# Feed-forward down products of a four-block network on one core: eight plain products per pair of blocks, or seven in Strassen's way

## Chip, cores and metric

The kernel runs on 1 core of one Trainium2 chip. The metric is the time of one execution on the device in microseconds; a comparison uses the median of the runs. Engines are named as the profile names them: PE (TensorE, matmuls), DVE (VectorE), ACT (ScalarE), POOL (GpSimd) and SP (SyncE, which issues the transfers here).

## What is computed

512 tokens of width 1024, float32, pass through two blocks of one kind (a mixer of three parts, layer norm, a feed-forward, layer norm) and two of another (feed-forward, attention mixer, feed-forward, gated side input, each with rms norms). The change concerns the feed-forwards alone:

```python
D_MODEL = 1024; D_FF = 4 * D_MODEL; D_FF_2 = 2816
# both layers of the first kind
h = layer_norm(DEEPNORM_ALPHA * h + mixed @ w_out[l], ln1_g[l], ln1_b[l])
ff = jnp.square(jax.nn.relu(h @ w_up[l])) @ w_down[l]
h = layer_norm(DEEPNORM_ALPHA * h + ff, ln2_g[l], ln2_b[l])
# twice in each layer of the second kind
def swiglu(x, wi, wo):
    gate, up = jnp.split(x @ wi, 2, axis=-1)
    return (jax.nn.silu(gate) * up) @ wo
```

So there are two feed-forwards of width 4096 (called FFN1 here) and four of width 2816 (FFN2(layer, first or second)).

## The kernel before, in words

**Products.** Every float32 operand of a matmul is split into a high part, rounded to the PE's float32r, and a low part, the difference; a product of two operands is three matmuls (`mm3`, L179 to L182): high x high, low x high, high x low. A weight tile of 128 x 1024 is a `unit` (L149 to L177): SP loads it into `raw`, ACT rounds it to `wh` (L143; with a gain vector L175), DVE makes `wl` (L144, or L176).

**Tokens.** The 512 tokens are four tiles t = 0 to 3. `h` and `acc` hold each as 128 x 1024. For an up product the input stands transposed in `xh`, `xl` (eight k tiles of 128 x 512 tokens): PE turns `h` against the identity into PSUM (`ax`, L255), ACT casts and DVE subtracts (L143, L144).

**FFN1** (`ffn1`, L449 on) goes through 8 groups of 512 hidden columns. `up` (L468 to L470) fills four PSUM banks; ACT applies Relu (L474), DVE squares (L475), and ACT and DVE split the result into `xh`, `xl` of a second transposed room. The down products of a group come one group later, while the next group's up products run: for each tile t and column half, 12 matmuls of 512 columns into one bank, which DVE adds to `acc` (L341; the first group takes the residual in, L359). The first group's up goes over the tokens in two halves (256 columns each), so that it can begin before the last two tiles are transposed. The last group's down goes tile by tile, and `done(t)` starts the norm of each tile as soon as it is there.

**FFN2** (`ffn2`, L495 on) is alike with 11 blocks of 256 hidden columns in groups [0], [1, 2], ... [9, 10]: up L516 to L518, Silu on ACT (L522), the product with the other half on DVE (L523).

**PSUM** has 8 banks: four `mm`, two `ax`, two `sx`. Weights rotate through 3 + 3 `raw` tiles and 4 + 2 pairs `wh`, `wl` inside the feed-forwards.

**Ends.** Behind an FFN2 `rms_add` (L430 to L438) computes `yg` = acc x gain on DVE, sums of squares on ACT (L402) and an inverse root in small DVE steps, then the new `h` in two halves (L437); `rms_T_late` transposes it. `ple` (L1252 on) is the gated side input: it loads `pt`, transposes it (L1261), and its gate is a down product of the whole `xh`, `xl` with `ple_gate_2`.

**Order.** The program is written in one sequence of operations; a list scheduler of the framework sets each engine's order from it, from dependencies and from the tiles' buffers. `issue_after` holds some weight splits back at a stage's start. So an order is known for each engine, and an instruction waits for semaphores in that order.

## Time and profile before

| | us |
|---|---|
| median of 3 runs (lowest, highest) | 3498.74 (3496.28, 3499.62) |
| the profiled execution's own time | 3504.65 |
| its span | 3502.9 |
| PE busy | 3444.0 (98%) |
| PE weight load busy | 2925.8 (84%) |
| DVE busy | 1843.2 (53%) |
| ACT busy | 1435.2 (41%) |
| DMA engines, mean busy share | 27.8% |

The span runs from the first to the last instruction of the profiled execution. Busy time adds up the durations of an engine's instructions, one on another counted once; matmuls overlap, so that a row's mean duration is not the distance of two starts. A group's idle time is that of its engine just before it, with what ended it. The chain of waits is followed back from the last instruction.

### The profile page before, as it was taken

To read this page: it belongs to the slowest core of one execution; us is meant where nothing else is said; L and a number is where in the kernel's file an instruction comes from. 1 tells how busy PE (TensorE), PEld (TensorE's weight loads), DVE (VectorE), ACT (ScalarE), POOL (GpSimd) and SP (SyncE) were. 2 spreads that over 40 slices of the span, in tenths; PEclk is the share of its full clock that TensorE was granted. 3 is DMA by queue.
4 is the path that set the end of the run, shared out by engine and by line. 5 is a ranking of instruction groups with operands and counts; after the bars stand their busy time and mean duration, and the time that the engine had idled before them with its cause. 6 is when DMAs were issued, how large, how long until landed. Compare 5 with 4: busy or idle time off the path is not lost.

```text
span 3502.9 us, 46155 instructions
## 1 busy us (share of the span) xinstructions
PE 3444.0 (98%) x17870; PEld 2925.8 (84%) x17870; DVE 1843.2 (53%) x4034; ACT 1435.2 (41%) x2529; POOL 11.2 (0%) x40
## 2 busy tenths in 40 slices
...
DMA packets 230512, 300.17 MB, mean 86 GB/s; under 512 B 23258, under 2 KB 148732, under 8 KB 230292
## 3 DMA queue, kind: packets, MB, share of 16 engines
q1 hardware_dynamic: 229716, 297.22, 27.8%
...
q14 instruction: 80, 0.66, 0.1%
q10 hardware_dynamic: 576, 0.00, 0.0%
...
## 4 chain that ended last, share of the span: by engine, by line
PE 92%; DVE 5%; ACT 2%; issue 1%; DMA 0%; SPq 0%; DVEq 0%; ACTq 0%
PE mm L180 14%; PE mm L181 14%; PE mm L182 14%; PE mm L516 9%; PE mm L517 9%; PE mm L518 9%; PE mm L469 3%; PE mm L470 3%; PE mm L468 3%; PE o L1014 2%; PE o L1148 1%; PE tp L609 1%; PE s L595 1%; PE o L1230 1%; PE ax L255 1%
## 5 line engine op out<-in xcount | busy, mean ns | idle before, releaser
L180 PE MATMUL mm<-wh,xh 128*128 128x512 f32 (+4 forms) x2496 | 939.6, 377 | 6.7 <-ACT wh L143 2.5
L181 PE MATMUL mm<-wh,xl 128*128 128x512 f32 (+4 forms) x2496 | 937.7, 376 | 0.0
L182 PE MATMUL mm<-wl,xh 128*128 128x512 f32 (+4 forms) x2496 | 937.7, 376 | 0.0
L144 DVE TENSOR_TENSOR wl<-raw,wh 128x1024 fp32r<-128x1024 f32 (+4 forms) x304 | 355.0, 1170 | 542.7 <-ACT wh L143 532.1
L143 ACT CAST wh<-raw 128x1024 fp32r<-128x1024 f32 (+4 forms) x304 | 306.3, 1009 | 758.9 <-PE mm L181 320.6
L175 ACT ACTIVATE wh<-raw,gT 128x512 fp32r<-128x512 f32 (+2 forms) x504 | 329.4, 697 | 618.3 <-issue 254.8
L516 PE MATMUL mm<-xh,wh 128*128 128x512 f32 (+1 forms) x1536 | 570.7, 373 | 2.2 <-ACT rl L522 1.6
L517 PE MATMUL mm<-xl,wh 128*128 128x512 f32 (+1 forms) x1536 | 571.9, 373 | 0.0
L518 PE MATMUL mm<-xh,wl 128*128 128x512 f32 (+1 forms) x1536 | 570.2, 373 | 1.3 <-DVE wl L176 1.3
L176 DVE SCALAR_TENSOR_TENSOR wl<-raw,gT,wh 128x512 fp32r<-128x512 f32 (+2 forms) x504 | 348.1, 723 | 423.2 <-ACT wh L175 422.6
L180 PEld LDWEIGHTS mm<-wh,xh 128*128 128x128 f32 x2496 | 473.8, 190 | 81.2 <-ACT xh L143 6.6
L181 PEld LDWEIGHTS mm<-wh,xl 128*128 128x128 f32 x2496 | 473.9, 190 | 71.4 <-DVE xl L144 1.0
L182 PEld LDWEIGHTS mm<-wl,xh 128*128 128x128 f32 x2496 | 473.3, 190 | 71.3 <-issue 1.4
L341 DVE TENSOR_TENSOR acc<-acc,mm 128x512 f32<-128x512 f32 x316 | 216.3, 685 | 244.8 <-PE mm L182 243.7
L516 PEld LDWEIGHTS mm<-xh,wh 128*128 128x128 f32 x1536 | 289.6, 189 | 54.5 <-ACT rl L522 2.4
L517 PEld LDWEIGHTS mm<-xl,wh 128*128 128x128 f32 x1536 | 290.9, 189 | 50.4 <-DVE xl L144 0.4
L518 PEld LDWEIGHTS mm<-xh,wl 128*128 128x128 f32 x1536 | 290.1, 189 | 51.3 <-DVE wl L176 1.5
L469 PE MATMUL mm<-xl,wh 128*128 128x512 f32 (+1 forms) x576 | 210.4, 366 | 1.5 <-DVE xl L144 1.5
L470 PE MATMUL mm<-xh,wl 128*128 128x512 f32 (+1 forms) x576 | 209.2, 366 | 0.1
L468 PE MATMUL mm<-xh,wh 128*128 128x512 f32 (+1 forms) x576 | 208.7, 366 | 0.0
L143 ACT CAST xh<-rl 128x512 fp32r<-128x512 f32 x152 | 93.4, 619 | 92.8 <-DVE rl L523 61.0
L469 PEld LDWEIGHTS mm<-xl,wh 128*128 128x128 f32 x576 | 108.6, 188 | 19.6 <-DVE xl L144 2.3
...
## 6 DMA issues: line engine op xcount, KB each, us to landing
...
raw<-ffn_wo SPq DMA_DIRECT2D x88, 512.0 KB, 3.8
raw<-w_up SPq DMA_DIRECT2D x64, 512.0 KB, 3.8
raw<-w_down SPq DMA_DIRECT2D x64, 512.0 KB, 3.7
...
raw<-w_out SPq DMA_DIRECT2D x16, 512.0 KB, 3.7
raw<-a_wqkv SPq DMA_DIRECT2D x16, 512.0 KB, 3.6
raw<-ple_gate SPq DMA_DIRECT2D x16, 512.0 KB, 3.6
```

The source lines that it names most:

```text
L143: act.copy(h, src)
L144: dve.tensor_tensor(l, src, h, OP.subtract)
L175: act.activation(wh[:, sl], v[:, sl], AF.Copy, scale=gv)
L176: dve.scalar_tensor_tensor(wl[:, sl], v[:, sl], gv, wh[:, sl], op0=OP.mult, op1=OP.subtract)
L180: pe.matmul(ps, sh, mh, start=start, stop=False)
L181: pe.matmul(ps, sl, mh, start=False, stop=False)
L182: pe.matmul(ps, sh, ml, start=False, stop=stop)
L469: pe.matmul(o, wh[:, j, fs_], xl, start=False, stop=False)
L470: pe.matmul(o, wl[:, j, fs_], xh, start=False, stop=k == 7)
L516: pe.matmul(o, wh[:, j, fs_], xh, start=k == 0, stop=False)
L517: pe.matmul(o, wh[:, j, fs_], xl, start=False, stop=False)
L518: pe.matmul(o, wl[:, j, fs_], xh, start=False, stop=k == 7)
```

## The change

Two blocks of 256 hidden columns make a pair, and a pair's down product is one product of block matrices, 2 x 2: token halves (tiles 0, 1 and 2, 3) by the two K halves of each block, times K halves by column halves of `w_down` or `ffn_wo_2`. `down7` computes it as seven products p1 to p7 of 12 matmuls each and not eight. The sums on the activations' side (S1 to S4) are four DVE operations of 256 columns per hidden tile pair and block (`pair_parts`, L474 to L477), the sums on the weights' side four of 1024 columns per pair (`minus`, L505, tiles `wt`), and each of the seven weight operands is split. p1 and p6 stay in the `ax` and `sx` banks over all pairs, p5 is summed in SBUF (`v5`); `share` adds the three into `acc` at the end. The other four products are added to `acc` per pair. A pair's down comes right behind its own up products.

FFN1: up goes by blocks of 256 (two PSUM banks, units of four k tiles x 256), the square is on ACT, 14 blocks go in seven pairs, the last two plainly in `last_group` (tiles 0, 1, then 2, 3, each pair over both blocks). FFN2: block 0 plain, 1 to 8 in four pairs, 9 and 10 in `last_group`. The extra room holds 3 pairs `wh`, `wl` and not 2. `ple` keeps its transposed side input in the room of `v5` and a `raw` tile. The counts of matmul instructions in the whole kernel go from 16826 to 16370: 360 fewer of 512 columns in the down products, and FFN1's two first up blocks as 192 of 256 and 96 of 512 columns where 384 of 256 stood, in each.

```diff
-XRAW, XWHL = 3, 2
+XRAW, XWHL = 3, 3
...
+    SLOT = 7 * 256
+    A12, A22, A11, S2, S3, S4, S1 = range(0, SLOT, 256)
...
+    def pair_parts(slot, ra, rb):
+        one, two = slice(0, 256), slice(256, 512)
+        split(*slot(A11, A11 + 256), ra[:, one])
+        split(*slot(A12, A12 + 512), rb)
+        dve.tensor_tensor(rb[:, two], rb[:, two], ra[:, two], OP.add)
+        dve.tensor_tensor(ra[:, two], ra[:, one], ra[:, two], OP.subtract)
+        dve.tensor_tensor(ra[:, one], rb[:, two], ra[:, one], OP.subtract)
+        dve.tensor_tensor(rb[:, one], rb[:, one], ra[:, one], OP.subtract)
+        split(*slot(S2, S2 + 512), ra)
+        split(*slot(S4, S4 + 512), rb)
...
+        return {1: [axt("p1", ax), axt("p1", ax)], 6: [axt("p6", sx), axt("p6", sx)], 5: v5, "begun": False}
...
+        def minus(x, y):
+            v = t_p.tile([128, 1024], F32, tag="t4", name="wt")
+            dve.tensor_tensor(v, x, y, OP.subtract)
+            return v
...
+        b11 = raw(0, 0)
+        u11 = parts(b11)
+        b21 = raw(1, 0)
+        u21 = parts(b21)
+        b12 = raw(0, 1)
+        t1 = minus(b12, b11)
+        b22 = raw(1, 1)
+        t2 = minus(b22, t1)
+        ut2 = parts(t2)
+        p2 = [mmt(), mmt()]
+        for i in range(2):
+            product(A11, u11, V[1], [i], not begun, last)
+            if i == 0:
+                product(S2, ut2, V[6], [i], not begun, last)
+            product(A12, u21, p2, [i])
+        product(S2, ut2, V[6], [1], not begun, last)
+        to_acc(p2, 0, 0)
+        ut1 = parts(t1)
+        p5 = [mmt(), mmt()]
+        product(S1, ut1, p5, (0, 1))
+        for tt in range(2):
+            v = V[5][:, tt]
+            if begun:
+                dve.tensor_tensor(v, v, p5[tt], OP.add)
+            else:
+                act.copy(v, p5[tt])
+        t4 = minus(b21, t2)
+        ut4 = parts(t4)
+        p4 = [mmt(), mmt()]
+        product(A22, ut4, p4, (0, 1))
+        to_acc(p4, 2, 0)
+        t3 = minus(b22, b12)
+        ut3 = parts(t3)
+        p7 = [mmt(), mmt()]
+        product(S3, ut3, p7, (0, 1))
+        to_acc(p7, 2, 1)
+        u22 = parts(b22)
+        p3 = [mmt(), mmt()]
+        product(S4, u22, p3, (0, 1))
+        to_acc(p3, 0, 1)
...
+    def last_group(hid, w, row0, done):
+        us = {(cc, u): unit(dap(w, (row0 + u * 256) * D + cc * 512, [[D, 128], [128 * D, 2], [1, 512]]), (2, 512))
+              for u in range(2) for cc in range(2)}
+        for t0 in (0, 2):
+            steps = [(t, cc) for t in (t0, t0 + 1) for cc in range(2)]
+            pss = {s: axt() if t0 == 0 and i < 2 else mmt() for i, s in enumerate(steps)}
+            for u in range(2):
+                for t, cc in steps:
+                    wh, wl = us[cc, u]
+                    for f in range(2):
+                        hh, hl = hid[2 * u + f]
+                        mm3(pss[t, cc], hh[:, t * 128:(t + 1) * 128], hl[:, t * 128:(t + 1) * 128],
+                            wh[:, f], wl[:, f], u + f == 0, u + f == 2)
+                    if u:
+                        sl = slice(cc * 512, cc * 512 + 512)
+                        dve.tensor_tensor(acc[t][:, sl], acc[t][:, sl], pss[t, cc], OP.add)
+                        if cc:
+                            done(t)
...
-        G = FF1 // 512
-        prev = None
-        for g in range(G):
-            cur = up(g, 2 if g == 0 else 1)
-            run_later()
-            if prev is not None:
-                dn(g - 1, prev)
-            prev = cur
-        dn(G - 1, prev)
...
+                act.activation(rl, rl, AF.Square)
...
+        for b in range(0, NB - 2, 2):
+            pair_parts(slot(0), *up(b, 1 if b else 2))
+            if not b:
+                run_later()
+            pair_parts(slot(1), *up(b + 1, 1))
+            V = V or sums(v5)
+            down7([slot(0), slot(1)], wd, (b, b + 1), V, init, b == NB - 4)
+        hid = [plain(i, r) for i, r in enumerate(up(NB - 2, 1))]
+        share(V, True)
+        hid += [plain(2 + i, r) for i, r in enumerate(up(NB - 1, 1))]
+        last_group(hid, wd, (NB - 2) * 256, done)
...
+        hid0 = [plain(4 + i, r) for i, r in enumerate(up(0, 2))]
+        V = None
+        for c in range(1, NB - 2, 2):
+            pair_parts(slot(0), *up(c, 1))
+            if c == 1:
+                for f in down_steps(hid0, wd, 0, True, False, init_copy, None, banks=[axt, axt]):
+                    f()
+                for t in (2, 3):
+                    dve.tensor_tensor(acc[t][:, 0:512], acc[t][:, 0:512], acc[t][:, 512:1024], OP.subtract)
+            pair_parts(slot(1), *up(c + 1, 1))
+            V = V or sums(v5)
+            down7([slot(0), slot(1)], wd, (c, c + 1), V, None, c == NB - 4)
+        hid = [plain(i, r) for i, r in enumerate(up(NB - 2, 1))]
+        share(V, False)
+        hid += [plain(2 + i, r) for i, r in enumerate(up(NB - 1, 1))]
+        last_group(hid, wd, (NB - 2) * 256, done)
...
-        pT = (ep.tile([128, 2, S], F32R, name="pTh"), ep.tile([128, 2, S], F32R, name="pTl"))
+        pT = (room.tile([128, 2, S], F32R, tag="v5", name="pTh"),
+              raw_tile(F32R).rearrange("p (k s) -> p k s", k=2))
```

In the listings below `h_97` to `h_100` are the tiles t = 0 to 3, `h<-h,g` multiplies a tile by the gain or adds the bias, `gv` is the transposed result with gain and bias, `bn`, `mv`, `rs...` are the norm's statistics.

**DVE at the start of layer 1's FFN1**, around the norm of the last tile. Before:

```order
L386 TENSOR_TENSOR h_99<-h_99,g_8591 128x1024 [waits DVE_49]
L199 SCALAR_TENSOR_TENSOR rsb_8814<-rsy_8813,rsp_8815 128x1 [waits DVE_49]
L204 SCALAR_TENSOR_TENSOR rsy_8813<-rsb_8814,rsy_8813 128x1 [waits DVE_49]
L199 SCALAR_TENSOR_TENSOR rsb_8814<-rsy_8813,rsq_8816 128x1 [waits DVE_49]
L204 SCALAR_TENSOR_TENSOR rsy_8813<-rsb_8814,rsy_8813 128x1 [waits DVE_49]
L379 TENSOR_SCALAR h_100<-acc_7953,mv_8807,rsy_8813 128x1024 [waits DVE_49]
L144 TENSOR_TENSOR wl_8968<-raw_8965,wh_8967 128x1024 [waits DMAHW5_49]
L144 TENSOR_TENSOR wl_9126<-raw_9123,wh_9125 128x1024 [waits DMAHW7_49]
L385 TENSOR_TENSOR h_100<-h_100,g_8589 128x1024 [waits DVE_49,PE_49]
L144 TENSOR_TENSOR xl_96<-gv_8830,xh_95 128x4x128 [waits Activation_49]
```

Now:

```order
L144 TENSOR_TENSOR wl_9184<-raw_9181,wh_9183 128x1024 [waits DMAHW4_49]
L208 SCALAR_TENSOR_TENSOR rsy_8985<-rsb_8986,rsy_8985 128x1 [waits DVE_49]
L505 TENSOR_TENSOR wt_9278<-raw_9276,raw_9264 128x1024 [waits DMAHW6_49,DMAHW0_49]
L203 SCALAR_TENSOR_TENSOR rsb_8986<-rsy_8985,rsq_8988 128x1 [waits DVE_49]
L505 TENSOR_TENSOR wt_9282<-raw_9280,wt_9278 128x1024 [waits DMAHW1_49,DVE_49]
L208 SCALAR_TENSOR_TENSOR rsy_8985<-rsb_8986,rsy_8985 128x1 [waits DVE_49]
L383 TENSOR_SCALAR h_100<-acc_8125,mv_8979,rsy_8985 128x1024 [waits DVE_49]
L144 TENSOR_TENSOR wl_9214<-raw_9211,wh_9213 128x1024 [waits DMAHW5_49]
L144 TENSOR_TENSOR wl_9267<-raw_9264,wh_9266 128x1024
L389 TENSOR_TENSOR h_100<-h_100,g_8761 128x1024 [waits DVE_49,PE_49]
L144 TENSOR_TENSOR wl_9273<-raw_9270,wh_9272 128x1024 [waits DMAHW7_49]
L144 TENSOR_TENSOR xl_96<-gv_9002,xh_95 128x4x128 [waits Activation_49]
```

A weight split of the second up block and two weight sums of the first pair stand ahead of `h_100`, and three weight splits, not two, between it and its first `xl`.

**PE at the passage from FFN2(0,1) to `ple(0)`**; `mm_20635` is the third product of the gate and `mm_21202` the first. Before, in the gate's third product:

```order
L180 MATMUL mm_20635<-wh_20606,xh_95 128x512
L255 MATMUL ax_20534<-cst_91,h_100 128x128 [waits DVE_49,PE_49]
L255 MATMUL ax_20534<-cst_91,h_100 128x128 x3
L1261 MATMUL ax_20573<-cst_91,pt_20569 128x128 [waits DMAHW7_49,PE_49]
L1261 MATMUL ax_20573<-cst_91,pt_20569 128x128
L255 MATMUL ax_20541<-cst_91,h_100 128x128 [waits DVE_49]
L255 MATMUL ax_20541<-cst_91,h_100 128x128 x3
L1261 MATMUL ax_20573<-cst_91,pt_20569 128x128 x2
L1261 MATMUL ax_20580<-cst_91,pt_20569 128x128 [waits PE_49]
L1261 MATMUL ax_20580<-cst_91,pt_20569 128x128 x3
L181 MATMUL mm_20635<-wh_20606,xl_96 128x512
```

Now, from the second turn of `h_99` on, which follows the last down product but for `h_99`'s first turn:

```order
L259 MATMUL ax_21089<-cst_91,h_99 128x128 [waits DVE_49,PE_49]
L259 MATMUL ax_21089<-cst_91,h_99 128x128 x3
L259 MATMUL ax_21150<-cst_91,h_100 128x128 [waits DVE_49,PE_49]
L259 MATMUL ax_21150<-cst_91,h_100 128x128 x3
L259 MATMUL ax_21157<-cst_91,h_100 128x128 [waits DVE_49,PE_49]
L259 MATMUL ax_21157<-cst_91,h_100 128x128 x3
L1423 MATMUL ax_21186<-cst_91,pt_21182 128x128 [waits DMAHW3_49,PE_49]
L1423 MATMUL ax_21186<-cst_91,pt_21182 128x128 x3
L1423 MATMUL ax_21193<-cst_91,pt_21182 128x128 [waits PE_49]
L1423 MATMUL ax_21193<-cst_91,pt_21182 128x128 x3
L184 MATMUL mm_21202<-wh_21205,xh_95 128x512 [waits Activation_49]
```

The gate's products stood around the transposes of `h_100` and `pt`, and now stand behind all of them.

**DVE behind the last up block of a pair**, FFN1 of layer 1; `rl` are the hidden values, `xl` with `rl` their low parts. Before, a group of 512 columns:

```order
L475 TENSOR_TENSOR rl_9091<-rl_9091 128x512 [waits Activation_49]
L475 TENSOR_TENSOR rl_9096<-rl_9096 128x512 [waits Activation_49]
L144 TENSOR_TENSOR wl_9279<-raw_9276,wh_9278 128x1024 [waits DMAHW3_49,PE_49,Activation_49]
L144 TENSOR_TENSOR xl_8857<-rl_9091,xh_8856 128x512 [waits Activation_49]
L144 TENSOR_TENSOR xl_8857<-rl_9096,xh_8856 128x512 [waits Activation_49]
L475 TENSOR_TENSOR rl_9101<-rl_9101 128x512 [waits Activation_49]
L475 TENSOR_TENSOR rl_9106<-rl_9106 128x512 [waits Activation_49]
L144 TENSOR_TENSOR xl_8857<-rl_9101,xh_8856 128x512 [waits Activation_49]
L144 TENSOR_TENSOR xl_8857<-rl_9106,xh_8856 128x512 [waits Activation_49]
```

Now, the pair's second block:

```order
L144 TENSOR_TENSOR xl_9029<-rl_9558,xh_9028 128x256 [waits Activation_49]
L144 TENSOR_TENSOR wl_9705<-raw_9592,wh_9704 128x1024 [waits PE_49,Activation_49]
L144 TENSOR_TENSOR xl_9029<-rl_9561,xh_9028 128x512 [waits Activation_49]
L474 TENSOR_TENSOR rl_9561<-rl_9561,rl_9558 128x256 [waits DVE_49]
L475 TENSOR_TENSOR rl_9558<-rl_9558 128x256 [waits DVE_49]
L476 TENSOR_TENSOR rl_9558<-rl_9561,rl_9558 128x256 [waits DVE_49]
L477 TENSOR_TENSOR rl_9561<-rl_9561,rl_9558 128x256 [waits DVE_49]
L144 TENSOR_TENSOR xl_9029<-rl_9558,xh_9028 128x512 [waits Activation_49]
L144 TENSOR_TENSOR xl_9029<-rl_9561,xh_9028 128x512 [waits Activation_49]
```

The squares are gone from DVE; between the first parts and the sums stand a weight split and the four sums, and the parts made of sums come last.

## Rows read from the trace of the kernel before

**Rows 1.** Page, span, busy time by engine, and the chain's shares by engine.

```profile
span 3502.9 us, 46155 instructions
PE 3444.0 (98%) x17870; PEld 2925.8 (84%) x17870; DVE 1843.2 (53%) x4034; ACT 1435.2 (41%) x2529; POOL 11.2 (0%) x40
...
PE 92%; DVE 5%; ACT 2%; issue 1%; DMA 0%; SPq 0%; DVEq 0%; ACTq 0%
```

**Rows 2.** Table by stage, feed-forwards: length, busy PE, PEld, DVE, ACT, POOL, clock, DMA share, GB/s.

```profile
317.00:675.00 358.00, 356.79 (x1675) 298.16 (x1673) 188.02 (x261) 119.31 (x172) 1.44 (x5) 1.00 0.31 95
...
sum 2188.00, PE 2182.23 PEld 1826.15 DVE 1043.15 ACT 765.85 POOL 1.77; mean PE 363.71 PEld 304.36 DVE 173.86 ACT 127.64 POOL 0.29
```

**Rows 3.** Page, costliest groups: matmul and weight load of line 180.

```profile
L180 PE MATMUL mm<-wh,xh 128*128 128x512 f32 (+4 forms) x2496 | 939.6, 377 | 6.7 <-ACT wh L143 2.5
...
L180 PEld LDWEIGHTS mm<-wh,xh 128*128 128x128 f32 x2496 | 473.8, 190 | 81.2 <-ACT xh L143 6.6
```

**Rows 4.** Timeline of PE in an FFN1 up stream: start, duration, instruction.

```profile
1482.69 0.39 PE L516 MATMUL mm<-xh,wh 128*128 128x512 f32 x1
1482.92 0.39 PE L517 MATMUL mm<-xl,wh 128*128 128x512 f32 x1
...
1483.37 0.39 PE L516 MATMUL mm<-xh,wh 128*128 128x512 f32 x1
```

**Rows 5.** Groups by shape, DVE, then ACT: busy us, mean ns, idle before.

```profile
L176 DVE SCALAR_TENSOR_TENSOR wl<-raw,gT,wh 128x512 fp32r<-128x512 f32 x440 | 314.3, 748 | 379.8 <-ACT wh L175 379.6
L144 DVE TENSOR_TENSOR wl<-raw,wh 128x1024 fp32r<-128x1024 f32 x256 | 312.9, 1224 | 482.1 <-ACT wh L143 476.3 <-DMA g<-ln_b 1.7 <-PE mm L182 0.6
L341 DVE TENSOR_TENSOR acc<-acc,mm 128x512 f32<-128x512 f32 x316 | 216.3, 685 | 244.8 <-PE mm L182 243.7
L144 DVE TENSOR_TENSOR xl<-rl,xh 128x512 fp32r<-128x512 f32 x152 | 104.1, 688 | 38.4 <-ACT xh L143 37.1
...
L143 ACT CAST wh<-raw 128x1024 fp32r<-128x1024 f32 x256 | 269.4, 1054 | 704.8 <-PE mm L181 269.4 <-PE mm L469 187.7 <-PE mm L517 168.5
L143 ACT CAST xh<-rl 128x512 fp32r<-128x512 f32 x152 | 93.4, 619 | 92.8 <-DVE rl L523 61.0 <-DVE rl L475 31.5
...
L474 ACT ACTIVATE rl<-mm 128x512 f32<-128x512 f32 x64 | 38.1, 595 | 13.8 <-PE mm L470 7.4 <-DVE xl L144 6.2
```

**Rows 6.** Table by stage, columns as in rows 2, behind PE's stop at 2060.

```profile
2060.40:2063.00 2.60, 2.42 (x10) 2.02 (x11) 1.91 (x4) 2.26 (x6) 0.00 (x0) 0.50 0.00 0
2063.00:2068.00 5.00, 5.00 (x32) 5.00 (x31) 4.72 (x21) 4.08 (x11) 0.00 (x0) 0.64 0.01 3
```

**Rows 7.** Timeline at layer 1's FFN1 start, PE, then DVE.

```profile
977.85 0.38 PE L469 MATMUL mm<-xl,wh 128*128 128x256 f32 x1 [0.58 <-DVE xl L144]
...
978.19 0.28 PE L468 MATMUL mm<-xh,wh 128*128 128x256 f32 x1
978.31 0.28 PE L469 MATMUL mm<-xl,wh 128*128 128x256 f32 x1
...
988.12 1.09 PE L255 MATMUL ax<-cst,h 128*128 128x128 f32 x8
...
987.25 0.81 DVE L379 TENSOR_SCALAR h<-acc,mv,rsy 128x1024 f32<-128x1024 f32 x1
...
993.12 0.68 DVE L144 TENSOR_TENSOR xl<-gv,xh 128x512 fp32r<-128x512 f32 x1
```

**Rows 8.** Timeline of PE, end of layer 1's FFN1.

```profile
1334.41 0.66 PE L255 MATMUL ax<-cst,acc 128*128 128x128 f32 x4 [3.10 <-ACT acc L415]
```

**Rows 9.** Timeline of PE, the gate's first and last matmul before t=3's transposes.

```profile
2430.73 0.48 PE L180 MATMUL mm<-wh,xh 128*128 128x512 f32 x1
...
2437.64 0.39 PE L180 MATMUL mm<-wh,xh 128*128 128x512 f32 x1
```

**Rows 10.** Page, DMA issues: KB each, median us to landing.

```profile
raw<-ple_gate SPq DMA_DIRECT2D x16, 512.0 KB, 3.6
...
pt<-p SPq DMA_DIRECT2D x2, 512.0 KB, 4.7
```

More of the change, by code (lines that the diff above doesn't have):

```diff
@@ L171, in unit @@
             else:
-                for i in range(2):
+                for i in range(na):
                     sl = slice(i * n, i * n + n)
@@ L315, in down_group, with down_steps @@
             step()
[L317 removed]
+    def down_steps(hid, w, row0, first, last, init, done, gi=None, us=None, banks=None):
         us = {} if us is None else us
@@ L454, in up, with ffn1 @@
+    def ffn1(l, xT, C, v5, done):
+        w, wd = a["w_up"][l], a["w_down"][l]
+        slot, plain = hid_room(C)
+        NB = FF1 // 256
+        def up(b, halves):
+            pss = [mmt() for _ in range(2)]
+            us = {}
             for hf in range(halves):
@@ L469, in up @@
                             pe.matmul(o, wh[:, j, fs_], xl, start=False, stop=False)
-                            pe.matmul(o, wl[:, j, fs_], xh, start=False, stop=k == 7)
-            hid = []
-            for f in range(4):
-                rl = tmp_p.tile([128, S], F32, tag="rl", name="rl")
+                            pe.matmul(o, wl[:, j, fs_], xh, start=False, stop=k == KT - 1)
+            rs = []
+            for f in range(2):
+                rl = t_p.tile([128, S], F32, tag="gv", name="rl")
```

179 lines of the change are left out of this document (105 added, 74 removed).

## The prediction

> **What bounds the kernel now.** I read the page's busy shares first [rows 1]: PE is busy 98% of the span of 3502.9 us, DVE 53%, ACT 41%, and the chain that ended last runs through PE for 92%. Then one table by stage [rows 2]: in the six feed-forward stretches, 2188.0 us together, PE idles 5.8 us, DVE is busy 1043.15 us (48%), and the clock is granted in full. So a feed-forward costs its matmul stream, and DVE has room. What a matmul costs is not what its row says: the group's mean is 377 ns [rows 3], but in a stream with no wait the first start lies at 1482.69, the second at 1482.92 and the fourth at 1483.37 [rows 4]: three slots in 0.68 us, 0.2267 us each. The durations overlap; the slot counts. Of 256 columns the starts lie 0.12 us apart [rows 7].
>
> The Trainium skill ("Trainium Kernel Development and Optimization", Performance Expectations) says the same in general: matmul busy time is a bad metric, because matmuls are pipelined. By durations the saving below would read 360 x 0.377 = 136 us; the starts above exclude it.
>
> **What the change removes.** Seven products of 12 matmuls replace 96: 84 a pair. There are 7 pairs in each FFN1 and 4 in each of four FFN2, 30 in all: 360 matmuls of 512 columns, x 0.2267 = **-81.6 us**. FFN1's first up block is cut in half-token passes for 256 columns of w_up, not 512: before 384 x 0.12 = 46.1 us, now 192 x 0.12 + 96 x 0.2267 = 44.8: -1.3, twice, **-2.6**.
>
> A removed matmul's slot has a floor in its weight load, 190 ns [rows 3]: 68.4 us. I keep the start distance, since the loads lie under it. The skill's "TensorE: Matmul & The Clock Gate" (Back-to-back issue gap) speaks against this change: it gives a stream of weight load and matmul pairs about 131 ns a matmul at 512 columns. By it the saving would be 47 us, and the edges below would make the kernel some 14 us slower. The 0.2267 of [rows 4] contradicts it here.
>
> **Inside a pair.** DVE in an FFN1 pair, at [rows 5]: eleven weight splits of 1.224, four weight sums at the same 1.224 (both are 1024-wide operations on two operands), ten evictions of 0.685, hidden parts 2 x (3 x 0.688 + 5 half-size operations at about 0.36, an estimate, half of 0.688): 13.5 + 4.9 + 6.9 + 7.7 = 33 us. PE has 96 + 84 = 180 matmuls, 40.8 us: DVE at 81%. FFN2: 62.6 us of PE and 16 x 0.748 + 8.6 + 4.9 + 2.8 + 7.7 + 6.9 = 43 us, 69%. ACT: 11 x 1.054 + 8 x 0.6 + hidden casts of 4.4 = 21 us, half. No engine passes PE, so I price the added DVE and ACT work inside pairs at nothing; its cover is the up stream. The tightest place is the down's 31st matmul (p6 with the second block's S2, 30 x 0.2267 = 6.8 us after the down begins), since the hidden sums follow the up directly now, where they had a whole group's time before. S2's chain [rows 5]: PE to ACT 0.4, Relu 0.6, square 0.6, cast and split of A12 1.3, four adds 1.4, cast and split 1.3: 5.6 us, and the third order listing puts one weight split (1.22) among them: 5.6 to 6.9. I take 6.5: no wait, with 0.3 us to spare.
>
> **The edges.** Here PE now waits.
> 1. *FFN1's start, twice.* Transposes of t=3 wait for h_100; ahead of them PE has the first half block. It was 96 matmuls of 256 columns (11.5 us), 977.85 to 988.12 [rows 7], and covered the layer-norm chain but for the 0.58 us. Now it is 48, 5.8 us: PE is there 5.8 us earlier. And three more 1024-wide operations of 1.22 us [rows 5] stand before h_100 in DVE's order (first listing), partly waiting for transfers: h_100 goes from 987.25 to some 991.4. PE waits 7 us. From h_100 to the second xl's end it was 6.6 us [rows 7]; one more weight split stands there now, and PE, its first half done, holds nothing else: 4 us more. **+11 each, 22** (bounds: 4, if the scheduler's order only looks late, to 14).
> 2. *Layer 1's FFN1 to FFN2(0,0).* last_group finishes the last two tiles 12 matmuls apart, 2.7 us, where tiles came every 24 (5.4). DVE chain of two tiles bunches. Now PE stops 3.10 us at 1334.41 [rows 8]; following DVE's rows I put the second half's begin 6 us later: **+6** (2.7 to 9). At the other FFN1's end **+2** (0 to 4).
> 3. *FFN2(0,0), (1,0), (1,1) ends*: the same bunching, 2.7 each: **+8** (0 to 12).
> 4. *FFN2(0,1) to ple(0).* Before, 31 matmuls of the gate, loaded early, started from 2430.73 to 2437.64 while t=3 was made [rows 9]. The second listing shows that the gate now stands behind all transposes, h_100 and pt. Let E be the last down matmul. h_99: add 0.7, yg 1.2, small operations 1.3, t=3's add and yg 1.9, two halves 1.5: E+6.6. h_100 hangs on its squares on ACT and comes 7 us later, E+13.7. The first gate weight's DMA is queued on SP behind pt, whose buffer comes free only at E+6.6; pt took 4.7 us to land and a gate load 3.6 [rows 10]: about E+12. ACT then has two squares, two xh, two pTh and the weight cast in two halves, eight 512-wide operations of about 0.7 us (an estimate between the 0.62 and 0.75 of such rows [rows 5]), 5.5 us, and DVE's first wl behind it: first gate matmul about E+20. The 24 transposes in it, 2.6 us, were there before. **+17** (8, if squares and casts overlap better, to 20).
> 5. *Clock.* In the 7.6 us behind the longest stop now, at 2060.4, the granted clock was 0.50 (1.2 GHz) for 2.6 us and 0.64 in the mean of the next 5.0 us: 1.3 + 1.8 = 3.1 us lost [rows 6]. Three new stops of that size (both FFN1 starts, ple): **+9** (0 to 15).
>
> Sum: -81.6 - 2.6 + 22 + 6 + 2 + 8 + 17 + 9 = **-20 us**. The profiled execution took 3504.65 us, so 3484.5; it stood 5.9 us over the median of 3498.74, so the forecast for a median is **3479**. The case's own range, edges within most of their bounds, is 3458 to 3494.
>
> **Rivals.**
> - *Edges mostly covered.* At their lower bounds they cost 8 + 2.7 + 0 + 0 + 8 + 0 = 19: -65, **3434 to 3456**. For it: stretches now idle 5.8 us in all [rows 2]. Against: both listings show shorter cover ahead of the same chains.
> - *S2 late in every pair (slower).* If DVE reaches the second block's S2 behind its evictions and weight splits, PE stops at the 31st matmul of each down. With the edges as above the change stops paying at 20 / 30 = 0.67 us a pair. A late split of 1.22 and one eviction more (0.69), less 0.3 spare, is 1.6 a pair: +48 - 20 = +28, **3527**; at 1.0 a pair it is 3509. For it: 81% DVE, and a spare of 0.3 us worked out from rows with no wait of its kind among them. Against: FFN2's pairs have 69%.
> - *Edges at their upper bounds*: 28 + 9 + 4 + 12 + 20 + 15 = 88: **3503**, no change.
> - *The change not doing what it says*: the listings count the removed matmuls; no chance.
>
> **Chances and range.** Forecast 0.54; edges covered 0.15; S2 late 0.20; edges at the top 0.10; saving by the page's rule 0.01. A measurement of this kernel tells about 0.2% (7 us) from no change. Faster by more: the covered case and nine tenths of the forecast, 0.64; within: the top case and the rest, 0.15; slower 0.21. The range goes from the covered case to the milder S2 case: 3434 to 3512.
>
> **What would show it.** Right: 84 matmul starts in 19.0 us in each pair's down, with no idle ahead of p6; ax<-h waits of 5 to 7 us on DVE at both FFN1 starts; a PE hole of 15 to 20 us before ple(0)'s gate with pt's transposes in it; a clock under 0.7 behind these. Wrong: waits of mm or p6 matmuls on xl<-rl in many pairs (S2), or edges without stops (covered).

## The result, and the profile after

| | us |
|---|---|
| after, median of 4 runs (lowest, highest) | 3461.6 (3457.01, 3467.13) |
| before, beside it, median of 4 runs | 3499.18 (3496.28, 3508.11) |
| after / before, 95% interval | 0.9889 (0.9865 to 0.9913) |
| the profiled execution of after, its own time | 3459.8 |

The change saves 37.6 us by the medians and 44.9 us between the two profiled executions; the latter pair is what the rows below explain. (Before's profiled run lay 5.5 us over its median here, after's 1.8 under.)

Span, busy time by engine and the chain's shares, page of after, beside [rows 1]:

```profile
span 3458.0 us, 46342 instructions
PE 3366.6 (97%) x17414; PEld 2854.9 (83%) x17414; DVE 2283.8 (66%) x4680; ACT 1638.9 (47%) x2831; POOL 11.2 (0%) x40
...
PE 88%; DVE 8%; ACT 3%; issue 1%; DMA 1%; SPq 0%; DVEq 0%; ACTq 0%
```

PE's busy time fell by 77.4 us, and the time in which PE is not busy (span less busy) rose from 58.9 to 91.4 us, by 32.5. The difference of the two is the 44.9. DVE took on 441 us of work and ACT 204, and neither shows as a cost of that size: they work beside PE. Who makes PE wait, in us, times and longest, from the lists of PE's waits, before and then after:

```profile
PE ax L255 <- ACT acc L415: 9.2, 5, 5.0
```

```profile
PE ax L259 <- DVE h L383: 13.2, 3, 6.7
PE ax L259 <- ACT acc L419: 12.1, 5, 6.1
PE ax L259 <- DVE h L441: 9.2, 3, 4.8
```

All three are transposes of a norm's result, at the ends of stages. The waits for `acc` were mostly there before (9.2 of 12.1 us); the waits for `h` are new, before they came to 0.3 us in all. Cutting both traces where a feed-forward's first up product starts gives the time by stage. "Slots" is the saving by counting matmuls: 12 x 0.2267 us a pair, and in each FFN1 0.64 us for its first two blocks (before 192 matmuls of 256 columns, 23.0 us; now 96 of 256 and 48 of 512, 22.4. The counts of 384, 192 and 96 given with the change are those of both FFN1 together). "Edge" is the rest.

| from first up product of | before | after | change | slots | edge | edge forecast |
|---|---|---|---|---|---|---|
| start of program to FFN1, layer 0 | 317.25 | 314.57 | -2.7 | 0 | (same code) | 0 |
| FFN1, layer 0, and a mixer | 659.51 | 647.39 | -12.1 | -19.7 | +7.6 | 16 |
| FFN1, layer 1 | 358.98 | 353.17 | -5.8 | -19.7 | +13.9 | 20 |
| FFN2(0,0) and mixer | 726.79 | 716.25 | -10.5 | -10.9 | +0.3 | 2.7 |
| FFN2(0,1) and `ple(0)` | 426.32 | 430.08 | +3.8 | -10.9 | +14.6 | 20 |
| FFN2(1,0) and mixer | 579.14 | 571.61 | -7.5 | -10.9 | +3.4 | 2.7 |
| FFN2(1,1), `ple(1)`, end | 434.9 | 424.9 | -10.0 | -10.9 | +0.9 | 2.7 |

(The forecast's 9 us for the clock is divided over the three edges that it named.) That the slots pay this is shown by the pairs below and by plain8; with it the edges cost 41 us in this pair of traces, not 64, and 45 us by the medians (82.9 less the 37.6 saved).

One trace gives a stage's length to a few us only. From a stop of PE in layer 0's mixer (at 718.19 before, 706.97 after) to layer 1's FFN1, code that the change does not touch, before took 258.6 us and after 255.0, and the other kept traces took 253.5 to 262.0. So 3.6 us of the second row's gain lie outside the change; up to that stop its edge is 11.1.

**Inside a pair.** PE's timeline of after in an FFN1 pair of layer 1: a pair's first `p` product, the one with S2 from the second block and the next, and the first `p` product of the next pair; then the DVE row of the S2 part.

```profile
1039.52 0.39 PE L184 MATMUL p<-wh,xh 128*128 128x512 f32 x1
...
1046.32 0.39 PE L184 MATMUL p<-wh,xh 128*128 128x512 f32 x1
1046.55 0.39 PE L185 MATMUL p<-wh,xl 128*128 128x512 f32 x1
...
1080.32 0.39 PE L184 MATMUL p<-wh,xh 128*128 128x512 f32 x1
```

```profile
1045.15 1.29 DVE L144 TENSOR_TENSOR xl<-rl,xh 128x512 fp32r<-128x512 f32 x2 [0.23 <-ACT xh L143]
```

Pairs begin 40.80 us apart, which is 180 x 0.2267, and PE is busy in all of it; DVE is busy 32.04 us (79%), and 41.24 of 62.56 us in an FFN2 pair (66%). ([Rows 4], from which the 0.2267 comes, are an FFN2 up stream, L516; FFN1's pairs keep the same distance.) The S2 product comes 6.80 us after the down begins and waits for nothing. Its low part is the first of the two operations of the DVE row and done at about 1045.84 (the second ends at 1046.44), 6.3 us after the down's start; the next matmul takes it at 7.03.

**The start of layer 1's FFN1**, PE's timeline, beside [rows 7]:

```profile
976.37 1.97 PE L259 MATMUL ax<-cst,h 128*128 128x128 f32 x8 [6.67 <-DVE h L383]
979.93 1.65 PE L624 MATMUL mm<-xh,wh 128*128 128x256 f32 x4 [1.60 <-ACT xh L143]
...
982.10 0.41 PE L624 MATMUL mm<-xh,wh 128*128 128x256 f32 x1
982.31 0.41 PE L625 MATMUL mm<-xl,wh 128*128 128x256 f32 x1
...
985.03 0.28 PE L624 MATMUL mm<-xh,wh 128*128 128x256 f32 x1
985.15 0.28 PE L625 MATMUL mm<-xl,wh 128*128 128x256 f32 x1
```

PE stops 6.67 us for `h_100`, then 1.60 for its transposed form. The 6.67 has two parts. PE runs out of work 7.74 us after the first up product (961.96 to 969.70); before, it came to the same transposes after 11.36 us (976.76 to 988.12), with 80 of the first half's 96 matmuls ahead of them, where 48 stand now. And `h_100` is done 14.35 us after the first up product, before 11.31. That is 3.6 us earlier and 3.0 later. The stop also shows in the pace: eight transposes take 1.97 us (1.09 in [rows 7]), and 256-column matmuls start 0.21 us apart at 982 and 0.12 again at 985. The table by stage (length, busy PE, PEld, DVE, ACT, POOL, granted clock, DMA share, GB/s) has the clock; 0.50 is 1.2 GHz:

```profile
976.40:980.00 3.60, 2.00 (x9) 1.60 (x9) 3.60 (x4) 2.56 (x8) 0.00 (x0) 0.50 0.32 88
980.00:985.00 5.00, 5.00 (x23) 4.35 (x24) 4.33 (x5) 1.56 (x4) 0.00 (x0) 0.59 0.94 319
985.00:990.00 5.00, 5.00 (x37) 4.70 (x36) 3.42 (x4) 3.95 (x6) 0.00 (x0) 1.00 0.11 40
```

Worked out as the prediction did it for [rows 6], this is 2.00 x 0.50 + 5.00 x 0.41 = 3.1 us lost to the clock, the 3 of the forecast (an estimate: some of it lies where PE would have waited in any case).

DVE, ahead of `h_100`:

```profile
971.71 1.21 DVE L144 TENSOR_TENSOR wl<-raw,wh 128x1024 fp32r<-128x1024 f32 x1
972.85 0.15 DVE L208 SCALAR_TENSOR_TENSOR rsy<-rsb,rsy 128x1 f32<-128x1 f32 x1
972.92 1.21 DVE L505 TENSOR_TENSOR wt<-raw 128x1024 f32<-128x1024 f32 x1
974.05 0.21 DVE L203 SCALAR_TENSOR_TENSOR rsb<-rsy,rsq 128x1 f32<-128x1 f32 x1
974.18 1.21 DVE L505 TENSOR_TENSOR wt<-raw,wt 128x1024 f32<-128x1024 f32 x1
...
975.50 0.81 DVE L383 TENSOR_SCALAR h<-acc,mv,rsy 128x1024 f32<-128x1024 f32 x1
```

One weight split and the two sums stand between the norm's small steps, as the listing of the order had it, each holding the next small step back by 1.1 us. No transfer is waited for.

**`ple(0)`**, PE's timeline, from the last down matmul to the gate's first:

```profile
2386.76 0.40 PE L186 MATMUL mm<-wl,xh 128*128 128x512 f32 x1
...
2391.97 1.94 PE L259 MATMUL ax<-cst,h 128*128 128x128 f32 x8 [4.82 <-DVE h L441]
2397.86 1.94 PE L259 MATMUL ax<-cst,h 128*128 128x128 f32 x8 [3.96 <-DVE h L441]
2399.59 1.56 PE L1423 MATMUL ax<-cst,pt 128*128 128x128 f32 x8
2402.45 0.50 PE L184 MATMUL mm<-wh,xh 128*128 128x512 f32 x1 [1.30 <-ACT wh L179]
```

4.82 + 3.96 + 1.30 = 10.1 us idle, where 31 matmuls of the gate stood before [rows 9]; the transposes between run at the low clock (eight in 1.94 us, 1.09 in [rows 7]; granted 0.50 from 2392 to 2398). From the down's end (2387.15) to the gate 15.3 us.

### The profile page after: what moved, and what is told of

Its sections match the earlier page's. It is cut to its first block, busy times and chain, and to the rows that moved or that the text cites. A ratio compares the mean times of both kernels' runs of the same rounds, so it can differ in the third digit from the quotient of the medians.

```text
span 3458.0 us, 46342 instructions
## 1 busy us (share of the span) xinstructions
PE 3366.6 (97%) x17414; PEld 2854.9 (83%) x17414; DVE 2283.8 (66%) x4680; ACT 1638.9 (47%) x2831; POOL 11.2 (0%) x40
## 4 chain that ended last, share of the span: by engine, by line
PE 88%; DVE 8%; ACT 3%; issue 1%; DMA 1%; SPq 0%; DVEq 0%; ACTq 0%
PE mm L184 11%; PE mm L186 11%; PE mm L185 11%; PE mm L681 9%; PE mm L680 9%; PE mm L682 9%; PE mm L625 3%; PE mm L626 3%; PE mm L624 3%; PE p L186 2%; PE p L185 2%; PE p L184 2%; PE o L1177 1%; PE tp L772 1%; PE o L1311 1%
## 5 line engine op out<-in xcount | busy, mean ns | idle before, releaser
L184 PE MATMUL mm<-wh,xh 128*128 128x512 f32 (+4 forms) x2072 | 773.1, 374 | 8.7 <-ACT wh L143 3.1
L186 PE MATMUL mm<-wl,xh 128*128 128x512 f32 (+4 forms) x2072 | 771.2, 373 | 2.2 <-DVE wl L180 2.2
L185 PE MATMUL mm<-wh,xl 128*128 128x512 f32 (+4 forms) x2072 | 771.6, 373 | 0.2 <-DVE xl L144 0.2
L682 PE MATMUL mm<-xh,wl 128*128 128x512 f32 (+1 forms) x1536 | 570.5, 372 | 1.3 <-DVE wl L180 1.3
L184 PEld LDWEIGHTS mm<-wh,xh 128*128 128x128 f32 x2072 | 393.3, 190 | 68.7 <-ACT xh L143 7.2
L681 PEld LDWEIGHTS mm<-xl,wh 128*128 128x128 f32 x1536 | 290.6, 189 | 50.7 <-DVE xl L144 1.0
L144 DVE TENSOR_TENSOR wl<-wt,wh 128x1024 fp32r<-128x1024 f32 x120 | 147.1, 1225 | 172.4 <-ACT wh L143 172.4
L143 ACT CAST wh<-wt 128x1024 fp32r<-128x1024 f32 x120 | 126.2, 1052 | 268.9 <-PE mm L681 163.1
L143 ACT CAST xh<-rl 128x512 fp32r<-128x512 f32 (+1 forms) x272 | 149.8, 573 | 202.1 <-DVE rl L476 134.6
L144 DVE TENSOR_TENSOR xl<-rl,xh 128x512 fp32r<-128x512 f32 (+1 forms) x272 | 166.1, 630 | 85.6 <-ACT xh L143 85.4
```

The source lines that it names most:

```text
L143: act.copy(h, src)
L144: dve.tensor_tensor(l, src, h, OP.subtract)
L184: pe.matmul(ps, sh, mh, start=start, stop=False)
L185: pe.matmul(ps, sl, mh, start=False, stop=False)
L186: pe.matmul(ps, sh, ml, start=False, stop=stop)
L681: pe.matmul(o, wh[:, j, fs_], xl, start=False, stop=False)
```

## The experiments

The theory: the removed matmuls pay 0.2267 us each and added vector work inside a pair is free; the losses lie at the edges, from FFN1's shorter first half, from the weight sums ahead of `h_100`, and from the gate standing behind `ple`'s transposes. Rivals: the slots pay less, with small edges; pairs sit on the brink of waiting for S2; the edges have other causes.

### plain8: eight products instead of seven, all else as after

```diff
-            pair_parts(slot(0), *up(b, 1 if b else 2))
+            q = b // 2 % 2 * 4
+            hid = [plain(q + i, r) for i, r in enumerate(up(b, 1 if b else 2))]
...
-            down7([slot(0), slot(1)], wd, (b, b + 1), V, init, b == NB - 4)
+            down_group(hid, wd, b * 256, b == 0, False, init_res, None, banks=[axt] * 8)
```

> The changed kernel with eight plain products (96 matmuls) in each of the 30 pairs where it has seven (84), everything else in its order: pairs still right behind their up products, FFN1 in blocks of 256, the same ends. Weight sums, hidden sums and the kept sums go with them. Theory (the gain is the matmul slots, DVE's added work is hidden, the edges cost what the trace of the changed kernel shows): 360 x 0.2267 = 81.6 us more than the changed kernel's 3461.6, 3543 (3537 to 3549), 44 us over the kernel before. Rival (a removed matmul gives back only its weight load, 190 ns): 68 us more, 3530. Rival (the seven products pay hidden stops inside pairs): less than 75 us more, under 3537.

3543.9 us (3540.26 to 3545.44), ratio to before 1.0125 (1.0109 to 1.0142). That is 82.3 us over after for 360 matmuls, 0.2286 us each: the start distance of [rows 4], not the 0.377 of the row. By the Trainium skill's 131 ns a matmul ("TensorE: Matmul & The Clock Gate", Back-to-back issue gap) it would have been 47 us, an estimate by that figure; the run decides against it for this stream. DVE is busy 1803.7 us in this kernel, 480 less than after, and the time shows none of it beyond the runs' scatter (81.6 expected for the slots alone): sums, splits and evictions inside a pair cost nothing that these runs can tell. The rest of the change, down right behind up and the new edges, costs 44.0 us over the before beside it, which agrees with the 45 above. PE's waits at the edges stand nearly as in after:

```profile
PE ax L259 <- ACT acc L419: 10.7, 4, 6.1
PE ax L259 <- DVE h L441: 10.5, 4, 4.8
PE ax L259 <- DVE h L383: 9.7, 2, 6.1
```

The stop at FFN1's start is 3.64 us at layer 0 (6.08 in after) and still 6.11 at layer 1 (6.67), though this kernel has no weight sums: at layer 1 two weight splits of the same 1.22 us stand on DVE ahead of `h_100` instead.

### two_blocks and two_blocks_b: FFN1's first half goes over two blocks

```diff
+            pre = None if b else up_mm((0, 1), 2)
-            pair_parts(slot(0), *up(b, 1 if b else 2))
+            pair_parts(slot(0), *up(b, 1, pre))
...
-            pair_parts(slot(1), *up(b + 1, 1))
+            pair_parts(slot(1), *up(b + 1, 1, pre))
```

`up_mm` is `up`'s matmul loop over a list of blocks, so that the first half has 96 matmuls of 256 columns and not 48. (In the trace of two_blocks_b 76 of them come ahead of `h_100`'s transposes at layer 1; the rest fills what was the second stop.)

> Alone: the first two blocks of each FFN1 go over the tokens in two halves together, so that 96 matmuls of 256 columns, not 48, stand ahead of the transposes of the last tile. Theory (short cover ahead of the norm of t=3): the waits on h at the two starts, 6.1 and 6.7 us with 1.6 behind each, shrink to 1 to 3 us, the clock behind them stays up (2 to 3 us each), 192 + 192 matmuls of 256 columns cost 1.3 us more each: 3461.6 - 14 = 3448 (3443 to 3453). Rival (the three 1024-wide operations ahead of h_100 on DVE set the stop and go on doing so): less than 5 us won, over 3456.

3769.22 us, ratio 1.0768, a miss by a slip: the other 28 blocks issued their up products twice. They are 28 x 48 = 1344 matmuls, 304.7 us at 0.2267; less these it is 3464.5. Its stops were already 2.72 and 3.30 us. With each issued once:

> As two_blocks, with every up product issued once (there, each of the other 28 FFN1 blocks was issued twice, 28 x 48 matmuls of 512 columns). Theory (cover): the stops ahead of h_100's transposes are 2.7 and 3.3 us as in two_blocks's trace, the 1.6 behind them go, 10 us of idle PE less; the half passes cost 2.6 more and part of the clock comes back: 3461.6 - 10 = 3452 (3446 to 3456). Rival (read from two_blocks's time, 3769.2 - 28 x 48 x 0.2267 = 3464.5): no gain; then what the shorter stop gives is lost behind it.

3450.95 us (3447.72 to 3455.22), ratio 0.9859 (0.9845 to 0.9874): 10.7 under after. PE's timeline at layer 1:

```profile
976.83 1.97 PE L259 MATMUL ax<-cst,h 128*128 128x128 f32 x8 [3.30 <-DVE h L383]
```

The shorter first half is a cause: half of the stop goes with it (2.72 us at layer 0, 3.30 at layer 1), and the stop of 1.60 behind the transposes goes whole. All four runs lie under all four of after. The clock falls behind the 3.30 too (the transposes still take 1.97).

### h100_first: the first pair's weight sums, and a weight split, behind h_100

```diff
-HOLD_LN = (-1, -1, 2, 3, 3, 3)
+HOLD_LN = (-1, -1, 3, 3, 3, 3)
...
+                for ins in V.get("after") or ():
+                    es.enter_context(tc.issue_after(ins))
+            V["after"] = None if b else mark[3]
```

`HOLD_LN` says behind which tile's norm a weight unit's split may be issued; the third unit, of the second up block, goes from `h_99` to `h_100`.

> Alone: the first pair's weight sums and the second up block's weight split of each FFN1 may be issued on DVE only behind h_100. Theory: h_100 comes three 1024-wide operations earlier, 3.4 us; the wait on h falls from 6.4 to 3 us at both starts: 3461.6 - 7 = 3455 (3451 to 3459). Rival (cover alone counts): no change.

3460.61 us (3455.91 to 3463.29), 0.9885 (0.987 to 0.99): the same as after. The stops did shrink, 6.08 to 1.77 at layer 0 and 6.67 to 3.63 at layer 1. PE's timeline and the table by stage, layer 1:

```profile
977.82 1.97 PE L259 MATMUL ax<-cst,h 128*128 128x128 f32 x8 [3.63 <-DVE h L383]
981.39 1.22 PE L627 MATMUL mm<-xh,wh 128*128 128x256 f32 x3 [1.60 <-ACT xh L143]
```

```profile
981.40:986.00 4.60, 4.60 (x18) 3.96 (x19) 4.60 (x6) 1.61 (x4) 0.00 (x0) 0.50 0.90 305
```

The clock stays at 0.50 for 4.6 us here (0.59 in after's 5 us), so that from the first up product to the first down product the gain is 2.1 us (36.8 to 34.6) for 3.0 us less of waiting. A gain of that size at two places lies inside the runs' scatter; whether the median holds it stays open. comb3, below, has the better evidence on the sums.

### fill: 48 matmuls by zero weights ahead of the transposes of h_100

```diff
+                            for _ in range(24 if halves == 2 and hf == 0 and k == KT - 1 else 0):
+                                pe.matmul(o[:64], zero, xh, start=False, stop=False)
```

They add zero to a sum, so that PE is busy in most of the stop.

> The changed kernel with 48 idle matmuls of 256 columns (zeros added to the first block's sums, 5.8 us) ahead of the transposes of the last tile at each FFN1 start: PE works through the stop and nothing else moves. Theory (a stop costs its idle time and then a lower clock behind it): h_100 comes when it came, the transposes take 1.0 us and not 2.0, the granted clock stays 1.00 behind them, the first down product comes 3 us earlier at each start (2 to 4): 3461.6 - 6 = 3456. Rival (the granted clock has nothing to do with the stop): no change in the distance from the first up product to the first down product, 36.8 us in layer 1.

3458.51 us (3457.61 to 3459.41), 0.988 (0.9864 to 0.9897): 3.1 under after and inside its scatter, where about 6 had been expected. PE's timeline, then the table by stage, layer 1:

```profile
977.83 1.09 PE L261 MATMUL ax<-cst,h 128*128 128x128 f32 x8 [0.99 <-DVE h L385]
980.94 1.05 PE L626 MATMUL mm<-xh,wh 128*128 128x256 f32 x4 [2.02 <-ACT xh L145]
```

```profile
977.80:981.00 3.20, 1.15 (x9) 0.92 (x9) 3.20 (x3) 2.61 (x8) 0.00 (x0) 1.00 0.21 54
981.00:985.00 4.00, 4.00 (x19) 3.64 (x20) 4.00 (x6) 1.57 (x4) 0.00 (x0) 0.58 1.01 318
```

The transposes run at the full clock, 1.09 us. But the second stop, 2.02 us with the eight transposes before it, brings the clock to 0.58 all the same. From the first up product to the first down product 36.8 became 35.9 us, and at layer 0 37.8 became 36.0. So PE's idling does cost clock; filling one stop of two gives back little.

### gate_first: ple's own load and transposes behind the first gate group

The edit moves the gate's `down_group` in `ple` ahead of the load and the transposes of `pt`.

> Alone: ple loads and turns its side input behind the first group of gate products in the program, so that the gate's weights are loaded and split ahead of it. Theory (the gate's products are the missing cover at ple(0)): of the three stops there, 4.8, 4.0 and 1.3 us, at most 2 stay, the clock behind them stays up (4 to 5 us), ple(1) is as it was: 3461.6 - 13 = 3449 (3444 to 3453). Rival (h_99 and h_100 are late by DVE's chain, and the gate only moves the stop to its third product): 5 us or less.

3461.73 us, 0.989 (0.9872 to 0.9908): no gain. At `ple(0)` the idle time fell from 10.1 to 2.49 + 2.79 us and the stage from 430.1 to 426.2; at `ple(1)`, which had no stop over 0.4 us, the same edit made some, and that stage is 4.0 us longer. PE's timeline, two places of `ple(0)`, two of `ple(1)`:

```profile
2401.34 0.52 PE L259 MATMUL ax<-cst,h 128*128 128x128 f32 x3 [2.49 <-DVE h L441]
...
2429.62 0.79 PE L184 MATMUL mm<-wh,pTh 128*128 128x512 f32 x1 [2.79 <-ACT wh L143]
...
3398.21 0.30 PE L259 MATMUL ax<-cst,h 128*128 128x128 f32 x1 [1.43 <-DVE h L441]
...
3415.75 0.50 PE L184 MATMUL mm<-wh,xh 128*128 128x512 f32 x1 [1.72 <-ACT wh L179]
```

### ple_own and ple_own_w: the low part of ple's input in a tile of its own

```diff
-XRAW, XWHL = 3, 3
+XRAW, XWHL = 2, 3
...
-              raw_tile(F32R).rearrange("p (k s) -> p k s", k=2))
+              room.tile([128, 2, S], F32R, tag="pTl", name="pTl"))
```

The change had put `pTl` into a `raw` tile, one of those through which the gate's weights come. One `raw` tile less pays for the room; the second kernel keeps the third and gives up a pair `wh`, `wl` (`XRAW, XWHL = 3, 2`).

> The changed kernel with the low part of ple's side input in a tile of its own, and not in one of the raw tiles; to make room, 5 raw tiles and not 6. Nothing in ple is moved in the program. The gate's weights are then queued and split ahead of the side input, and 35 gate products stand on PE ahead of h_100's transposes, as in the kernel before. Theory (the raw tile that the side input takes puts the gate behind it): the stops at ple(0), 10.1 us, fall to 1 or 2, the clock behind them stays up, FFN2(0,1)'s start to FFN2(1,0)'s start takes 416 us and not 430; ple(1) and the pairs are as they were: 3461.6 - 14 = 3448 (3444 to 3453). Rival (as gate_first showed: the stop goes on to a later place): 427 us or more, 3458 and over. Rival (5 raw tiles starve the pairs): stops on wh in pairs.

> As ple_own, with the room taken from the weight pairs: 6 wh, wl (the number before the change) and 6 raw tiles. Theory (seven splits in a down need the seventh pair): each down's later products wait for a split, 0.5 to 1 us a pair, 15 to 30 us over ple_own: 3463 to 3478. Rival (six are enough): as ple_own, 3448.

3452.57 us (3449.29 to 3456.57), 0.9867 (0.9852 to 0.9882), and 3453.31 (3452.2 to 3455.24), 0.987 (0.9854 to 0.9887): 9.0 and 8.3 us under after. The gate's products stand ahead of `h_100`'s transposes again, as before the change, with nothing moved in the program's text, and the stage takes 422.0 us, where 416 was expected. Most of the difference is one stop and the clock behind it: PE waits 2.51 us for `h_100`, and from 2403.5 to 2410 the granted clock is 0.74, some 1.7 us of the 6.5. On DVE four of the gate's weight splits, 0.75 us each, now stand among the steps of `h_100`'s norm. PE's timeline of ple_own; the second row is a new stop of `ple(1)`, whose stage is 2.0 us longer than in after:

```profile
2403.50 0.30 PE L259 MATMUL ax<-cst,h 128*128 128x128 f32 x1 [2.51 <-DVE h L441]
...
3395.69 0.30 PE L259 MATMUL ax<-cst,h 128*128 128x128 f32 x1 [2.53 <-DVE h L441]
```

So with `pt` at its place in the program it was the tile of the weight ring that held the gate behind the transposes: it is all that the two kernels have in common against after. Five raw tiles or six pairs `wh`, `wl` are enough for the stream, whose pairs still begin 40.8 and 62.6 us apart in both (two FFN1 pairs of ple_own_w 40.87).

### late3: three idle DVE operations ahead of each pair's second sums

```diff
+        for _ in range(idle):
+            dve.tensor_tensor(rb, rb, rb, OP.max)
...
-            pair_parts(slot(1), *up(b + 1, 1))
+            pair_parts(slot(1), *up(b + 1, 1), idle=3)
```

> The changed kernel with three more 512-wide DVE operations (the maximum of the second block's hidden values with themselves) ahead of the sums of each pair's second block. In the changed kernel S2's last part is there 6.32 us after the down's start in FFN1 and 5.65 in FFN2, and it is wanted at 7.03. Theory (the wait at the 31st matmul has 0.7 and 1.4 us to spare, and past that every pair pays): three operations of 0.69 put S2 2.1 us later, FFN1's 14 pairs pay 1.4 each, FFN2's 16 pairs 0.7: 3461.6 + 31 = 3493 (3484 to 3502), with waits on xl<-rl at p6. Rival (DVE's free 20 to 30% hides it): under 5 us, 3466.

3470.71 us (3467.38 to 3473.01), 0.9914 (0.9899 to 0.9929): 9.1 over after where 31 had been expected: about 0.3 us a pair (pairs begin 41.1 and 62.85 us apart, from 40.8 and 62.6: 0.3 x 14 + 0.25 x 16 = 8), and not a wait of 1 us in each. The scheduler set S2's product among the first ones of p5 (PE's timeline):

```profile
1055.56 0.39 PE L184 MATMUL mm<-wh,xh 128*128 128x512 f32 x1
1055.80 0.73 PE L184 MATMUL p<-wh,xh 128*128 128x512 f32 x2
1056.37 0.40 PE L185 MATMUL mm<-wh,xl 128*128 128x512 f32 x1
```

A late S2 was a real cost, but one that the order gives way to: other products of the pair don't need S2. The scheduler set this order for a program in which the three operations stand; a delay of S2 in an order set without it was not tried.

### by_tile: the last group tile by tile

```diff
-            for u in range(2):
-                for t, cc in steps:
+            for u, (t, cc) in ([(u, s) for u in range(2) for s in steps] if t0 == 0 else
+                               [(u, s) for t in (2, 3) for u in range(2) for s in steps if s[0] == t]):
```

> Alone: last_group's tiles 2 and 3 go one after the other (both blocks of tile 2, then of tile 3), so that tile 2 is done 5.4 us ahead of the end and not 2.7. Theory (the two last tiles' norms bunch on DVE): the stop at the start of FFN2(0,0) falls from 6.07 us to 3.5, the first one at ple(0) from 4.8 to 2, the stop of 2.0 at mixer b (2822) is no more than that: 3461.6 - 6 = 3456 (3452 to 3460). Rival (the last tile alone sets these stops): no stop changes by over 0.5 us.

3461.61 us (3458.58 to 3462.8), 0.9888 (0.9873 to 0.9902): no change. The stop at FFN2(0,0) went from 6.07 us to 0.73 and 4.88, the one at `ple(0)` from 4.82 to 5.33; one behind FFN2(1,0), for a weight split, from 2.01 to 0.70. PE's timeline of by_tile:

```profile
1316.82 0.48 PE L259 MATMUL ax<-cst,acc 128*128 128x128 f32 x1 [4.88 <-ACT acc L419]
```

That the last two tiles end close together is at most a small part of the first two stops. It has a part in the third, which is also gone in ple_own_w, with one pair `wh`, `wl` less.

### comb2 and comb3: the parts that helped, together

comb2 is two_blocks_b with h100_first and ple_own. comb3 is two_blocks_b with ple_own_w, and of h100_first the weight sums alone (`HOLD_LN` as in after).

> two_blocks_b, h100_first and ple_own together. Theory (the edges are independent): 10.7 less by two_blocks_b, 14 by ple_own, and the 2.7 and 3.3 us left at FFN1's starts fall to under 1 with h100_first, 4 more: 3461.6 - 29 = 3433 (3428 to 3440). Rival (what one edge gives back is lost behind it): over 3443.

> two_blocks_b and ple_own_w together, and the first pair's four weight sums (these alone, not the up blocks' splits, which made the first half's cover shorter in comb2) only behind h_100. Theory (cover and the queue ahead of h_100 were the two causes at FFN1's start, the raw tile the one at ple(0)): no stop over 1 us ahead of h_100's transposes in FFN1, one of 2.5 at ple(0): 3451.0 - 8.3 by ple_own_w, 5 to 7 less at the two starts: 3437 (3432 to 3443). Rival (as comb2: the parts give back less together): 3445 and over.

comb2: 3448.59 us (3446.36 to 3450.27), 0.9855 (0.984 to 0.9869), where 3433 was expected. At layer 1 PE still stops 3.56 us: holding the third weight unit behind `h_100`, beside the fourth, leaves only 52 of the first half's 96 matmuls ahead of it. comb3 lets the third go behind `h_99` again, and 76 stand ahead: 3436.37 us (3431.72 to 3440.85), ratio **0.9815** (0.9802 to 0.9829), 25 us under after and the fastest of all. If what two_blocks_b and ple_own_w save alone adds up, they make 3442.7; comb3 lies 6.3 below that, all five of its runs under it, and has the sums behind `h_100` on top. So the sums seem to cost some 6 us once the first half is longer; that the two parts add up was not tried by itself. Page and PE's waits of comb3:

```profile
PE 3369.8 (98%) x17510; PEld 2862.7 (83%) x17510; DVE 2277.6 (66%) x4680; ACT 1639.6 (48%) x2831; POOL 11.2 (0%) x40
```

```profile
PE ax L259 <- ACT acc L419: 12.1, 5, 6.1
PE ax L259 <- DVE h L441: 5.0, 2, 2.5
...
PE ax L259 <- DVE h L383: 2.2, 2, 1.8
```

The waits for L383, 13.2 us in after, are down to 2.2, and those for L441 from 9.2 to 5.0.

## Why the prediction was right, and where its sums were off

The forecast, 3479 us and faster, had direction and mechanism right and half of the size: 20 us of saving, and 37.6 came by the medians (44.9 in the profiled pair).

- **The slots** (-81.6): right. plain8 gives 82.3 in the medians. The -2.6 beside it is counted twice over: 384 matmuls of 256 columns are those of both FFN1, so that the term is 0.64 each and -1.3 in all.
- **Inside a pair at nothing**: right, by the 40.80 us between pairs and by plain8's 480 us less DVE work without a gain beyond the slots. DVE's share was put at 81 and 69% and is 79 and 66%. S2 was taken to be ready 6.5 us after the down begins, for 6.8; in an FFN1 pair it is there at about 6.3 and its low part is needed only at 7.03, since the products with the high part go first.
- **The step that was off: the sizes of the edges**, 64 us in the sum (22 + 6 + 2 + 8 + 17 + 9), 41 in the traces and 45 by the medians. Three terms:
  - *FFN1's start*, 11 each and 3 for the clock. The first stop is 6.67 us where 7 was said, which is luck: PE "5.8 us earlier" and `h_100` 4.15 later (987.25 to 991.4) would make 10, and the 7 has no working. Both parts were too large, 3.6 and 3.0 in the trace. Before, 80 matmuls and not 96 stood ahead of the transposes (977.85 to 988.12 is 10.3 us, not 11.5), and no transfer was waited for. And "4 us more" behind `h_100` was wrong: the second stop is 1.60 us, because the first matmuls of the second half need only `xh`, and DVE's splits run beside them. In layer 1 the start costs 10.4 us where 14 was said, and the end 3.4, not 6; in layer 0 both cost 11.1, not 16. (The cuts are where PE stops ahead of FFN2(0,0), and the stop in layer 0's mixer.)
  - *`ple(0)`*, 17 and 3. `h_100` was set at E+13.7 and the gate at E+20; they came at E+11.2 and E+15.3. Behind `h_100` the sum had 6.3 us, with eight ACT operations of 0.7 and the gate's first `wl`; it was 4.1, since ACT's operations are shorter and the gate's first matmul waits for `wh` alone (the 1.30 in its row). 14.6 us, not 20.
  - *Bunching at the FFN2 ends*, 2.7 each. They show 0.3, 3.4 and 0.9, 4.6 in all and not 8; of the 3.4, 2.01 us are a stop that by_tile brings to 0.70, so there the cause has a part. Where FFN1 passes to FFN2(0,0) the stop did grow, to 6.07 us from the 3.10 of [rows 8], but by_tile leaves 5.61 of it in two: the cause given, tiles that end 12 matmuls apart, is not the main one, and what it is stays open.
- **The causes** behind the two large edges were right: the shorter first half (two_blocks_b, -10.7), the gate behind all transposes (ple_own, -9.0), and the 1024-wide DVE operations ahead of `h_100`. These last shorten the stops when moved (h100_first) but show in the time only together with the longer first half (comb3, some 6 us); in plain8 weight splits in their place do the same at layer 1. For the gate the prediction saw the order but not its reason, the `raw` tile.
- **The rival of a late S2** had its place right and its price too high: late3 delays S2 by three DVE operations and loses 0.3 us a pair, not over 1, because the order takes another product meanwhile. That is half of the break-even of 0.67 us a pair, with the delay put in on purpose.
- Of the 44.9 us of the profiled pair, 2.7 lie ahead of the first FFN1 and 3.6 in layer 0's mixer, in code that the change doesn't touch. Without them it is 38.6, close to the 37.6 of the medians.

Left open: the stop ahead of FFN2(0,0), 6.07 us in every kept trace of the changed kernel but by_tile's; whether the weight splits among `h_100`'s steps are the whole of the 2.5 us that stay at `ple(0)`; how much of the edges the clock holds for itself, beyond the estimate above, since fill takes away only one stop of two.
